# Layer B's attention scores: from 128-row products to pairs of 64-row products

## The chip, the cores and the metric

One core of one Trainium2 chip runs the whole program. The metric is device time in microseconds (us), one launch, the median of the runs. TensorE (PE in the profile) multiplies and loads its weights (PEld), VectorE (DVE), ScalarE (ACT) and GpSimd (POOL) do the rest, and SyncE (SP) issues most of the transfers.

## The reference

Two transformer layers over 512 tokens of width 1024, each with a gate and sandwich norms: layer A is latent attention, layer B differential attention with 8 heads. What matters here is the inner part of layer B. Each head has two halves of 64 dimensions, each half its own scores and its own softmax:

```python
scale = DIFF_QK ** -0.5                       # DIFF_QK = 64
s1 = jnp.einsum('bqhd,bkhd->bhqk', qa, k1).astype(jnp.float32) * scale
s2 = jnp.einsum('bqhd,bkhd->bhqk', qb, k2).astype(jnp.float32) * scale
p = masked_softmax(s1, mask) - lam_full * masked_softmax(s2, mask)
return jnp.einsum('bhqk,bkhe->bqhe', p.astype(v.dtype), v)
```

The mask is causal in chunks of 64 tokens, so a block of 128 queries i needs the keys of the blocks 0 to i only: 128, 256, 384 and 512 of them.

## The kernel before

Every float32 operand is split into a high part and a low remainder (`split`), both in the type that TensorE takes in one pass, and a product is summed from three or four such parts. The layers follow each other: layer A (to about 386 us in the profile), then layer B's attention, then its output projection.

In layer B the query and key projections are made feature-major, split, and stored part by part to two scratch arrays in DRAM, `scratch["q"]` and `scratch["k"]`, with the axes half-head, 64 rows, high or low part, 512 tokens (`to_scratch`). `load_head` (L893) gathers them again. For each half g it loads one tile `q` whose 128 rows are 64 rows of the high and the low part in turn, and two tiles `kh` and `kl`, in which each of the 64 rows of the key's high or low part stands twice. So two products over 128 rows,

```python
pe.matmul(o[:, :n], q[:, ti], kh[:, :n], start=True, stop=False)
pe.matmul(o[:, :n], q[:, ti], kl[:, :n], start=False, stop=True)
```

sum all four part products of one half. `scores_b` (L905) does that for the four query blocks and both halves: 16 products a head, each into a PSUM bank of its own by query block and half, so 8 of the 8 banks pass through a head. The tiles come from a pool `hd` of 8 buffers of 256 KB; a head takes six of them.

`softmax_part` (L515) follows each product with one DVE reduction (L526: mask, scale, copy to SBUF, running extreme, then a short instruction that reads the accumulator into `mx`) and one ACT exponential (L529). `eb`, `mxb` belong to the first half, `ec`, `mxc` to the second. The two halves are combined at L925 and L926.

The order on PE is written out by hand (`pe_order`), the other engines' orders come from the framework's scheduler. `attention_b` (L955) issues the scores of head h+1, then `fill`s of half a projection unit each (12 products of 512 columns) taken from the remaining key, query and gate projections, then the transposes of head h, more fills, the norm's sum of head h-1 (`subln`, a product into the bank `ssb`) and head h's product with the values (`pv`). `BESIDE` says how many half units go where; the first of its three numbers is a `gap` that `softmax_part` calls between the second and the third query block of the scores, so one half unit stands in the middle of a head's scores for heads 1 to 6 (and head 0). Head 7 has none. The weights of the units are split ahead on POOL (high part) and DVE (low part, `wl`, 128x1024); the output projection's second half has the same for `w1h` and `w1l`.

Of the kernel before, what the change touches and what calls it, by code (L numbers as in the profile page):

```python
# [20 lines left out]
P = 128  # L21
# [4 lines left out]
H = 8  # L26
# [3 lines left out]
SCALE_B = 64 ** -0.5  # L30
# [27 lines left out]
def f(ap):  # L58
    return ap.bitcast(F32)
# [84 lines left out]
def body(tc, ins, outs, dbg=None):  # L144
    nc = tc.nc
    ctx = ExitStack()
    with ctx:
        _body(ctx, tc, nc, ins, outs, dbg or {})


def _body(ctx, tc, nc, ins, out, dbg):
# [14 lines left out]
    act, dve, gps, pe = nc.scalar, nc.vector, nc.gpsimd, nc.tensor  # L166

    def ps(name):
        return psp.tile([P, 512], F32, tag="ps", name=name)

    def big_t(name, dt=F32R):
        return big.tile([P, 8, 512], dt, tag="big", name=name)

    def hd_t(name, dt=F32R):
        return hd.tile([P, 512], dt, tag="hd", name=name)

    def tmp_t(name, dt=F32):
        return tmp.tile([P, 512], dt, tag="tmp", name=name)
# [4 lines left out]
    def sm_t(name, n=4, bufs=None):  # L183
        return sm.tile([P, n], F32, tag=name, name=name, bufs=bufs)
# [161 lines left out]
    for kc in range(KC):  # L346
# [4 lines left out]
        g = [ws.get()]  # L351
# [8 lines left out]
        for m in range(5):  # L360
            gh, gl = g[1 if kc == 0 and m else 0]
            k = m - 1 if kc == 0 and m else m
# [74 lines left out]
    for m in range(4):  # L437
        t = tmp_t("cn")
# [38 lines left out]
    for n in range(2):  # L477
        o = [ps(f"va{n}_{i}") for i in range(NT)]
        for p in range(2):
            wh, wl = ws.get()  # L480
            for i in range(NT):
                ti = slice(i * P, i * P + P)
# [29 lines left out]
            qk[nm, h] = (hi, lo)  # L512
        ws.ahead()

    def softmax_part(h, tags, srcs, nscale, gap=None):  # L515

        e = [epool.tile([P, 1280], F32, tag="e", name=f"e{tag}{h}") for tag in tags]
        st = [[sm_t(n + tag) for n in ("mx", "l", "ri")] for tag in tags]
        for i in range(NT):
            n = P * (i + 1)  # L520
            one = slice(i, i + 1)
            for et, (mx, l, _), src in zip(e, st, srcs):
                ev = et[:, OFF[i]:OFF[i] + n]
                o = src(i)

                last = dve.tensor_tensor_reduce(  # L526
                    out=ev, in0=o[:, :n], in1=mask[:, 512 - n:], op0=ALU.add, op1=ALU.min, scalar=-3 * NEG,
                    scale=nscale if isinstance(nscale, float) else nscale[:, one], accum_out=mx[:, one])
                act.activation(ev, ev, AF.Exp, bias=mx[:, one], scale=-1.0, accum_out=l[:, one])  # L529
            if gap and i == 1:  # L530
                gap()
        behind[h] = last.ins
        for _, l, ri in st:
            dve.reciprocal(ri, l)  # L534
        return [(et, x[2]) for et, x in zip(e, st)]
# [26 lines left out]
    def transposes(h):  # L562
        e = es.pop(h)
        b = [ps(f"pt{h}_{k}") for k in range(3)]
        where = [(b[0], 0), (b[1], 0), (b[2], 0), (b[1], 384)]
        for i in range(NT):
            for j in range(i + 1):
                t, o = where[j]
                pe.transpose(t[:, o + (i - j) * P:o + (i - j) * P + P],  # L569
                             e[:, OFF[i] + j * P:OFF[i] + j * P + P], ident)  # L570
        ph = ptp.tile([P, 1280], F32R, tag="pt", name=f"pth{h}")
        pl = ptp.tile([P, 1280], F32R, tag="pt", name=f"ptl{h}")
        for k, (o, n) in enumerate(((0, 512), (512, 512), (1024, 256))):
            split(nc, ph[:, o:o + n], pl[:, o:o + n], b[k][:, :n])
        return ph, pl
# [15 lines left out]
    def split_og(zg, ogh, ogl, hs):  # L591
        for h in hs:
            split(nc, ogh[:, h], ogl[:, h], zg[:, h])
# [51 lines left out]
    def wo_pair(q):  # L645
        w = ws.get()
        for h in (2 * q, 2 * q + 1):
            wo_half0(w, h, range(NT))
        ws.ahead()
        for _ in range(2 if q == 2 else 1):  # L650
            ws.get()
            ws.ahead()
# [175 lines left out]
    scratch = {nm: drp.tile([2 * H, 64, 2, 512], F32, name=f"{nm}dr") for nm in "qk"}  # L828
# [43 lines left out]
    def unit(nm, m):  # L872

        x = (hT1h, hT1l) if nm == "k" else (hT2h, hT2l)
        w = ws.get()
        o = ps(f"{nm}b{m}")
        for kc in range(KC):
            if kc == KC // 2:
                yield
            mm3(o, (w[0][:, kc], w[1][:, kc]), (x[0][:, kc], x[1][:, kc]), kc == 0, kc == KC - 1)  # L880
        ws.ahead()
        evac(nm, m, o)
        yield

    halves = (None for nm, m in beside for _ in unit(nm, m))

    def fill(n):
        for _ in range(n):
            next(halves)

    heads = {}

    def load_head(h, nms="kq"):  # L893
        for g in range(2):
            t = heads.setdefault((h, g), {})
            if "q" in nms:
                t["q"] = hd_t(f"q{g}")
                nc.sync.dma_start(f(t["q"][:]), scratch["q"][2 * h + g].rearrange("r n t -> (r n) t"))
            if "k" in nms:
                for n, nm in enumerate(("kh", "kl")):  # L900
                    t[nm] = hd_t(f"{nm}{g}")
                    nc.sync.dma_start(f(t[nm][:]),
                                      scratch["k"][2 * h + g, :, n].unsqueeze(1).to_broadcast([64, 2, 512]))

    def scores_b(h, gap):  # L905
        hg = [[heads[h, g][nm] for nm in ("q", "kh", "kl")] for g in range(2)]
        second = {}

        def src(i):


            n = P * (i + 1)
            ti = slice(i * P, i * P + P)
            os = [ps(f"sb{h}_{g}_{i}") for g in range(2)]
            for o, (q, kh, kl) in zip(os, hg):
                pe.matmul(o[:, :n], q[:, ti], kh[:, :n], start=True, stop=False)
                pe.matmul(o[:, :n], q[:, ti], kl[:, :n], start=False, stop=True)
            second[i] = os[1]
            return os[0]

        (e1, r1), (e2, r2) = softmax_part(h, "bc", [src, second.get], -SCALE_B, gap)
        dve.tensor_scalar(r2, r2, lam_c, None, op0=ALU.mult)
        for i in range(NT):
            w = slice(OFF[i], OFF[i] + P * (i + 1))
            act.activation(e2[:, w], e2[:, w], AF.Copy, scale=r2[:, i:i + 1])  # L925
            dve.scalar_tensor_tensor(e1[:, w], e1[:, w], r1[:, i:i + 1], e2[:, w],  # L926
                                     op0=ALU.mult, op1=ALU.subtract)
        es[h] = e1
# [3 lines left out]
    def subln_sq(h, o):  # L932
        sq = tmp_t("sqo")
        act.activation(sq, o, AF.Square)
        if h < H - 1:
            ob[h] = tmp_t("sqh", F32R), tmp_t("sql", F32R)
            split(nc, *ob[h], sq)
        else:
            ob[h] = sq,
        dve.scalar_tensor_tensor(zg[:, h], o, gsub, zg[:, h], op0=ALU.mult, op1=ALU.mult)  # L940

    def subln(h):
        b = ps(f"ssb{h}")
        parts = ob.pop(h)
        for n, t in enumerate(parts):
            pe.matmul(b, ones_r if len(parts) > 1 else ones, t, start=n == 0, stop=n == len(parts) - 1)
        rs = tmp_t("rs")
        act.activation(rs, b, AF.Ln, bias=eps_c, scale=1.0 / 128)
        act.activation(rs, rs, AF.Exp, scale=-0.5)
        (dve if h > 4 else gps).tensor_tensor(zg[:, h], zg[:, h], rs, op=ALU.mult)  # L950


    BESIDE = [(1, 2, 2), (1, 2, 3), (1, 2, 1), (1, 2, 2), (1, 1, 1), (1, 1, 2), (0, 0, 0)]

    def attention_b():  # L955
        pt = {}
        scores_b(0, lambda: fill(1))
        load_head(1)
        fill(4)
        for h in range(H):  # L960
            a, b, c = BESIDE[h] if h + 1 < H else (0, 0, 0)
            if h + 1 < H:
                scores_b(h + 1, lambda: fill(a))
                fill(b)
                if h + 2 < H:
                    load_head(h + 2)
            if h == 5:
                st["og"] = big_t("ogh"), big_t("ogl")
            if h == 6:
                w1[0], w1[1] = st["w1"] = big_t("w1h"), big_t("w1l")  # L970
                st["acc"] = [ps(f"wo0_{i}") for i in range(NT)]
                wo_pair(0)
            pt[h] = transposes(h)
            fill(c)
            if h == 6:
                subln(5)
                split_og(zg, *st["og"], [5])
                wo_pair(1)
            elif h == 7:
                wo_pair(2)  # L980
            elif h:
                subln(h - 1)
                if h == 5:
                    split_og(zg, *st["og"], range(5))
            subln_sq(h, pv(h, pt.pop(h)))
# [117 lines left out]
```

## Time and profile before

| what | value |
|---|---|
| median of 3 runs | 578.09 us (578.03 to 578.71) |
| the profiled execution | 576.0 us, of which the span from first to last instruction is 574.1 us |
| granted TensorE clock | 0.998 over the span; 1.00 from 386 to 535 us |
| DVE, ACT, POOL busy | 63%, 44%, 24% of the span |
| layer B's score products | 386.2 to 515 us, 128 products |

A row of the timeline has the start and the length of an instruction in us, its engine, line, operation, the tiles it writes and reads, and shapes. PE's products overlap: what one costs in a dense stretch is the distance from its start to the next start, not its length. A bracket gives the idle time before it and who ended it.

### The profile page before, as it was taken

Reading aid. Unit: us, or ns where it says so; the run is one execution under the profiler, and the core shown is the slowest. Engines: PE = TensorE matmul, PEld = TensorE weight load, DVE = VectorE, ACT = ScalarE, POOL = GpSimd, SP = SyncE. Lnnn points to the kernel's source line nnn. Section 1 sums busy time; section 2 is a strip of 40 time slices with the busy share of each in tenths; the row PEclk is TensorE's granted clock in tenths of the full one; section 3 lists DMA queues with packets and bytes.
Section 4 is the critical chain, followed back from the end, with each engine's and each line's share of the span. In section 5 each row is a group of like instructions: output and inputs, shape, how many; then the busy total and the mean of one; then the engine's idle time right before and its main releaser. Section 6 shows DMA issues by size and latency. Waiting matters only on the chain.

```text
span 574.1 us, 7800 instructions
## 1 busy us (share of the span) xinstructions
PE 565.5 (98%) x2749; PEld 477.4 (83%) x2749; DVE 362.5 (63%) x728; ACT 252.0 (44%) x560; POOL 139.9 (24%) x191
## 2 busy tenths in 40 slices
PE   8999999999999999999999999999999999999995
PEld 7888888888888888888888888888888888888785
DVE  6839845335566665856786575436666667687554
ACT  6146152222244344331476130124674695986432
POOL 1044402012232323321122332332223223243000
PEclk9999999999999999999999999999999999999999
DMA  8356576655544335697741377845755745557012
GB/s 303 104 180 184 185 231 192 217 165 132 168 131 125 97 104 165 208 375 259 237 147 47 110 202 224 288 130 189 250 172 179 238 130 181 187 168 253 1 58 90
DMA packets 39334, 100.54 MB, mean 175 GB/s; under 512 B 4592, under 2 KB 5248, under 8 KB 39296
## 3 DMA queue, kind: packets, MB, share of 16 engines
q1 hardware_dynamic: 26048, 57.16, 29.2%
q0 software_dynamic: 12624, 41.97, 24.4%
q10 hardware_dynamic: 624, 0.92, 0.6%
q8 instruction: 22, 0.36, 0.3%
q14 instruction: 16, 0.13, 0.1%
HBM read 86.66 MB, written 12.58 MB: 173 GB/s over the span
## 4 chain that ended last, share of the span: by engine, by line
PE 90%; DMA 3%; issue 2%; DVE 2%; POOL 1%; ACT 0%; DVEq 0%; POOLq 0%
PE wo L194 4%; PE wo L192 4%; PE wo L193 4%; PE za L192 3%; PE zb L192 3%; PE zb L193 3%; PE qb L194 3%; PE kb L193 3%; PE kb L194 3%; PE kb L192 3%; PE qb L193 3%; PE vb L194 3%; PE za L193 3%; PE vb L193 3%; PE vb L192 3%; PE za L194 3%
## 5 line engine op out<-in xcount | busy, mean ns | idle before, releaser
L116 DVE TENSOR_TENSOR wl<-wr,wh 128x1024 fp32r<-128x1024 f32 (+2 forms) x44 | 46.9, 1067 | 50.7 <-DMA wh<-in_w_uv 7.5
L138 POOL TENSOR_SCALAR wh<-wr 128x1024 fp32r<-128x1024 f32 x30 | 33.4, 1113 | 78.3 <-PE zb L193 26.7
L141 DVE TENSOR_TENSOR wl<-wr,wh 128x1024 fp32r<-128x1024 f32 x32 | 39.0, 1219 | 17.1 <-POOL wh L138 17.0
L136 ACT ACTIVATE pth<-pt 128x512 fp32r<-128x512 f32 (+1 forms) x48 | 22.3, 525 | 17.6 <-PE pt L569 17.4
L141 DVE TENSOR_TENSOR ptl<-pt,pth 128x512 fp32r<-128x512 f32 (+1 forms) x48 | 26.3, 593 | 4.2 <-ACT pth L136 3.8
L529 ACT ACTIVATE ea<-ea,mxa 128x128 f32<-128x128 f32 (+3 forms) x32 | 18.0, 561 | 22.9 <-DVE mxa L526 22.8
L557 POOL TENSOR_SCALAR ea<-ea,ria 128x128 f32<-128x128 f32 (+3 forms) x32 | 16.9, 541 | 41.7 <-DVE ria L534 41.7
L192 PE MATMUL wo<-w1h,ogh 128*128 128x512 f32 (+1 forms) x72 | 26.8, 372 | 0.0
L193 PE MATMUL wo<-w1l,ogh 128*128 128x512 f32 (+1 forms) x72 | 26.4, 367 | 0.0
L194 PE MATMUL wo<-w1h,ogl 128*128 128x512 f32 (+1 forms) x72 | 26.4, 366 | 0.0
L194 PE MATMUL wo<-wh,ogl 128*128 128x512 f32 x64 | 24.9, 392 | 0.3 <-DVE ogl L141 0.3
L192 PE MATMUL zb<-hT2h,wh 128*128 128x512 f32 x64 | 25.3, 395 | 0.0
L192 PE MATMUL kb<-hT1h,wh 128*128 128x512 f32 x64 | 25.1, 393 | 0.0
L193 PE MATMUL wo<-wl,ogh 128*128 128x512 f32 x64 | 25.0, 391 | 0.0
L192 PE MATMUL za<-xh,wh 128*128 128x512 f32 x64 | 25.0, 391 | 0.0
L194 PE MATMUL zb<-hT2h,wl 128*128 128x512 f32 x64 | 25.0, 391 | 0.0
L192 PE MATMUL qb<-hT2h,wh 128*128 128x512 f32 x64 | 25.0, 391 | 0.0
L193 PE MATMUL zb<-hT2l,wh 128*128 128x512 f32 x64 | 25.0, 390 | 0.0
L194 PE MATMUL qb<-hT2h,wl 128*128 128x512 f32 x64 | 24.9, 390 | 0.0
L193 PE MATMUL kb<-hT1l,wh 128*128 128x512 f32 x64 | 24.9, 390 | 0.0
L194 PE MATMUL kb<-hT1h,wl 128*128 128x512 f32 x64 | 24.9, 390 | 0.0
L193 PE MATMUL qb<-hT2l,wh 128*128 128x512 f32 x64 | 24.9, 389 | 0.0
(347 smaller groups left out, 1707.4 us busy)
## 6 DMA issues: line engine op xcount, KB each, us to landing
wr<-in_w_za SPq DMA_DIRECT2D x8, 512.0 KB, 3.9
wh<-in_w_za POOLq DMA_DIRECT2D x8, 512.0 KB, 4.2
wr<-in_w_oa SPq DMA_DIRECT2D x8, 512.0 KB, 4.4
wr<-in_w_qb POOLq DMA_DIRECT2D x8, 512.0 KB, 5.1
kh<-kdr SPq DMA_DIRECT2D x16, 256.0 KB, 4.0
kl<-kdr SPq DMA_DIRECT2D x16, 256.0 KB, 4.0
q<-qdr SPq DMA_DIRECT2D x16, 256.0 KB, 3.7
wr<-in_w_zb POOLq DMA_DIRECT2D x8, 512.0 KB, 3.9
```

What stands on the lines that cost most here:

```text
L116: self.nc.vector.tensor_tensor(lo, raw, f(hi), op=ALU.subtract)
L136: nc.scalar.activation(hi, src, AF.Copy)
L138: nc.gpsimd.tensor_scalar(hi, src, 1.0, 1.0, op0=ALU.mult, op1=ALU.mult)
L141: (nc.vector if lo_eng == "dve" else nc.gpsimd).tensor_tensor(lo, src, f(hi), op=ALU.subtract)
L192: pe.matmul(o, w[0], x[0], start=first, stop=False)
L193: pe.matmul(o, w[0], x[1], start=False, stop=False)
L194: pe.matmul(o, w[1], x[0], start=False, stop=last)
L529: act.activation(ev, ev, AF.Exp, bias=mx[:, one], scale=-1.0, accum_out=l[:, one])
L557: gps.tensor_scalar(ev, ev, ri[:, i:i + 1], 1.0, op0=ALU.mult, op1=ALU.mult)
```

## The change

`load_head` loads plain rows: per head two tiles for q and two for k, one of the high and one of the low parts, with half 0 in rows 0 to 63 and half 1 in rows 64 to 127. `scores_b` makes three products a query block and half (high by high, low by high, high by low; the product of the two low parts is no longer summed), each over 64 rows, the two halves in turn: half 0 on the rows 0 to 63 of the array, half 1 on the rows 64 to 127. The products of the query blocks 0 and 1 (128 and 256 columns) of a half share one PSUM bank, `two[g]`, so a head takes six banks. The gap is gone: a head's four query blocks follow each other, and `BESIDE` keeps the number of fills between one head's scores and the next.

```diff
-    def softmax_part(h, tags, srcs, nscale, gap=None):
+    def softmax_part(h, tags, srcs, nscale):
...
-            if gap and i == 1:
-                gap()
...
     def load_head(h, nms="kq"):
-        for g in range(2):
-            t = heads.setdefault((h, g), {})
-            if "q" in nms:
-                t["q"] = hd_t(f"q{g}")
-                nc.sync.dma_start(f(t["q"][:]), scratch["q"][2 * h + g].rearrange("r n t -> (r n) t"))
-            if "k" in nms:
-                for n, nm in enumerate(("kh", "kl")):
-                    t[nm] = hd_t(f"{nm}{g}")
-                    nc.sync.dma_start(f(t[nm][:]),
-                                      scratch["k"][2 * h + g, :, n].unsqueeze(1).to_broadcast([64, 2, 512]))
-
-    def scores_b(h, gap):
-        hg = [[heads[h, g][nm] for nm in ("q", "kh", "kl")] for g in range(2)]
-        second = {}
+
+        t = heads.setdefault(h, {})
+        for nm in nms:
+            src = scratch[nm][2 * h:2 * h + 2].rearrange("g r n t -> (g r) n t")
+            t[nm] = hd_t(f"{nm}h"), hd_t(f"{nm}l")
+            for n in range(2):
+                nc.sync.dma_start(f(t[nm][n][:]), src[:, n])
+
+    def scores_b(h):
+        t = heads.pop(h)
+        (qh, ql), (kh, kl) = t["q"], t["k"]
+        halves = [slice(64 * g, 64 * g + 64) for g in range(2)]
+        second, two = {}, [ps(f"sb{h}_{g}_01") for g in range(2)]
...
-            os = [ps(f"sb{h}_{g}_{i}") for g in range(2)]
-            for o, (q, kh, kl) in zip(os, hg):
-                pe.matmul(o[:, :n], q[:, ti], kh[:, :n], start=True, stop=False)
-                pe.matmul(o[:, :n], q[:, ti], kl[:, :n], start=False, stop=True)
+            os = [two[g][:, P * i:P * i + n] if i < 2 else ps(f"sb{h}_{g}_{i}")[:, :n] for g in range(2)]
+            for a, (q, k) in enumerate(((qh, kh), (ql, kh), (qh, kl))):
+                for o, rs in zip(os, halves):
+                    pe.matmul(o, q[rs, ti], k[rs, :n], start=a == 0, stop=a == 2)
...
-    BESIDE = [(1, 2, 2), (1, 2, 3), (1, 2, 1), (1, 2, 2), (1, 1, 1), (1, 1, 2), (0, 0, 0)]
+    BESIDE = [(3, 2), (3, 3), (3, 1), (3, 2), (2, 1), (2, 2), (0, 0)]
...
-        scores_b(0, lambda: fill(1))
+        scores_b(0)
         load_head(1)
-        fill(4)
+        fill(5)
...
-                scores_b(h + 1, lambda: fill(a))
-                fill(b)
+                scores_b(h + 1)
+                fill(a)
```

On PE only the score products change their place and number; every other PE instruction keeps its order. The first place is PE at the scores of head 0, query blocks 0 and 1 (`sb_0` and `sb_1` are the two halves' banks, the bracket names what an instruction waits for). Before:

```order
L916 MATMUL sb_0_0_3414<-kh_3102,q_3270 128x128 [waits DMAHW2_49,DMAHW0_49]
L917 MATMUL sb_0_0_3414<-kl_3104,q_3270 128x128 [waits DMAHW3_49]
L916 MATMUL sb_1_0_3415<-kh_3106,q_3272 128x128 [waits DMAHW4_49,DMAHW1_49]
L917 MATMUL sb_1_0_3415<-kl_3108,q_3272 128x128 [waits DMAHW5_49]
L916 MATMUL sb_0_1_3424<-kh_3102,q_3270 128x256
L917 MATMUL sb_0_1_3424<-kl_3104,q_3270 128x256
L916 MATMUL sb_1_1_3425<-kh_3106,q_3272 128x256
L917 MATMUL sb_1_1_3425<-kl_3108,q_3272 128x256
```

After this, half a unit of `kb` followed. With the change:

```order
L913 MATMUL sb_0_01_3402<-kh,qh 128x128 [waits DMAHW6_49,DMAHW2_49]
L913 MATMUL sb_1_01_3403<-kh,qh 128x128
L913 MATMUL sb_0_01_3402<-kh,ql 128x128 [waits DMAHW7_49]
L913 MATMUL sb_1_01_3403<-kh,ql 128x128
L913 MATMUL sb_0_01_3402<-kl,qh 128x128 [waits DMAHW3_49]
L913 MATMUL sb_1_01_3403<-kl,qh 128x128
L913 MATMUL sb_0_01_3402<-kh,qh 128x256 [waits DVE_49]
L913 MATMUL sb_1_01_3403<-kh,qh 128x256 [waits DVE_49]
L913 MATMUL sb_0_01_3402<-kh,ql 128x256
L913 MATMUL sb_1_01_3403<-kh,ql 128x256
L913 MATMUL sb_0_01_3402<-kl,qh 128x256
L913 MATMUL sb_1_01_3403<-kl,qh 128x256
```

Eight products have become twelve, in pairs, and the first 256-column product of each half now waits for DVE, in head 0 as in every head. By the semaphore's count in the built program it is the accumulator read (`mxb`, and `mxc` for the second half) of the reduction of query block 0, which reads the same bank.

The second place is DVE at the scores of head 7 with the change. These rows stood in the same order before:

```order
L141 TENSOR_TENSOR w1l<-wr_4661,w1h 128x1024
L141 TENSOR_TENSOR w1l<-wr_4861,w1h 128x1024
L526 ISA eb_4768,mxb<-sb_0_01_4766,mask 128x128
L526 ISA mxb 128x1
L526 ISA ec_4769,mxc<-sb_1_01_4767,mask 128x128
L526 ISA mxc 128x1
L526 ISA eb_4768,mxb<-sb_0_01_4766,mask 128x256
```

Nothing moved here; two splits of the output projection's weights stand ahead of the reductions, and PE now waits for the second and the fourth of the rows after them.

## Rows read from the trace of the kernel before

**Rows 1.** The page, busy time by engine, and the chain's shares by engine.
```profile
PE 565.5 (98%) x2749; PEld 477.4 (83%) x2749; DVE 362.5 (63%) x728; ACT 252.0 (44%) x560; POOL 139.9 (24%) x191
...
PE 90%; DMA 3%; issue 2%; DVE 2%; POOL 1%; ACT 0%; DVEq 0%; POOLq 0%
```

**Rows 2.** The view of waits, PE alone: us in total, times, longest.
```profile
PE warm L291 <- DVE ones L279: 1.1, 1, 1.1
PE g L366 <- ACT xh L348: 0.5, 1, 0.5
PE wo L194 <- DVE ogl L141: 0.3, 1, 0.3
PE sa L194 <- DVE qnl L141: 0.2, 1, 0.2
```

**Rows 3.** Timeline of PE, head 1's scores: where each query block starts.
```profile
402.43 0.22 PE L916 MATMUL sb<-kh,q 128*128 128x128 f32 x1
...
402.83 0.33 PE L916 MATMUL sb<-kh,q 128*128 128x256 f32 x1
...
403.35 0.40 PE L192 MATMUL zb<-hT2h,wh 128*128 128x512 f32 x1
...
406.10 0.33 PE L916 MATMUL sb<-kh,q 128*128 128x384 f32 x1
...
406.81 0.40 PE L916 MATMUL sb<-kh,q 128*128 128x512 f32 x1
...
407.73 0.40 PE L192 MATMUL zb<-hT2h,wh 128*128 128x512 f32 x1
```

**Rows 4.** Timeline of PEld, head 0: weight loads of 128-column products.
```profile
386.34 0.19 PEld L916 LDWEIGHTS sb<-kh,q 128*128 128x128 f32 x1
...
386.45 0.19 PEld L917 LDWEIGHTS sb<-kl,q 128*128 128x128 f32 x1
```

**Rows 5.** Timeline, head 0: first half's last 128-column product, then both reductions.
```profile
386.29 0.28 PE L917 MATMUL sb<-kl,q 128*128 128x128 f32 x1
...
386.60 0.29 DVE L526 CUSTOM_DVE_ANT_0 eb<-sb,mask 128x128 f32<-128x128 f32 x1 [0.21 <-PE sb L917]
...
386.82 0.09 DVE L526 DVE_READ_ACCUMULATOR2_ANT mxb<- 128x1 f32 x1
...
387.04 0.08 DVE L526 DVE_READ_ACCUMULATOR2_ANT mxc<- 128x1 f32 x1
```

**Rows 6.** Timeline, output projection: a PE product released by DVE.
```profile
533.41 0.40 PE L193 MATMUL wo<-wl,ogh 128*128 128x512 f32 x1
...
533.41 0.68 DVE L141 TENSOR_TENSOR ogl<-zb,ogh 128x512 fp32r<-128x512 f32 x1
...
534.15 0.50 PE L194 MATMUL wo<-wh,ogl 128*128 128x512 f32 x1 [0.34 <-DVE ogl L141]
```

**Rows 7.** Timeline, head 7: the splits on DVE, the first product, the first reduction.
```profile
510.90 3.20 DVE L141 TENSOR_TENSOR w1l<-wr,w1h 128x1024 fp32r<-128x1024 f32 x2 [1.31 <-POOL w1h L138]
...
512.13 0.28 PE L916 MATMUL sb<-kh,q 128*128 128x128 f32 x1
...
514.02 0.28 DVE L526 CUSTOM_DVE_ANT_0 eb<-sb,mask 128x128 f32<-128x128 f32 x1
```

**Rows 8.** The chain that ended last, 510 to 534 us: its longest pieces.
```profile
514.40 6.26 DMA wr<-in_w_ob
...
521.72 6.81 DMA wr<-in_w_ob
...
533.49 0.61 DVE ogl L141
```

**Rows 9.** Timeline of PE: ten transposes between units, an edge of another kind of product.
```profile
412.97 0.39 PE L194 MATMUL zb<-hT2h,wl 128*128 128x512 f32 x1
413.20 1.25 PE L569 MATMUL pt<-ident,eb 128*128 128x128 f32 x10
414.21 0.48 PE L192 MATMUL kb<-hT1h,wh 128*128 128x512 f32 x1
414.52 0.39 PE L193 MATMUL kb<-hT1l,wh 128*128 128x512 f32 x1
```

More of the change, by code (lines that the diff above doesn't have):

```diff
@@ L913, in src @@
             ti = slice(i * P, i * P + P)
-            os = [ps(f"sb{h}_{g}_{i}") for g in range(2)]
-            for o, (q, kh, kl) in zip(os, hg):
-                pe.matmul(o[:, :n], q[:, ti], kh[:, :n], start=True, stop=False)
-                pe.matmul(o[:, :n], q[:, ti], kl[:, :n], start=False, stop=True)
+            os = [two[g][:, P * i:P * i + n] if i < 2 else ps(f"sb{h}_{g}_{i}")[:, :n] for g in range(2)]
+            for a, (q, k) in enumerate(((qh, kh), (ql, kh), (qh, kl))):
+                for o, rs in zip(os, halves):
+                    pe.matmul(o, q[rs, ti], k[rs, :n], start=a == 0, stop=a == 2)
             second[i] = os[1]
             return os[0]
-        (e1, r1), (e2, r2) = softmax_part(h, "bc", [src, second.get], -SCALE_B, gap)
+        (e1, r1), (e2, r2) = softmax_part(h, "bc", [src, second.get], -SCALE_B)
         dve.tensor_scalar(r2, r2, lam_c, None, op0=ALU.mult)
@@ L950, in subln @@
         (dve if h > 4 else gps).tensor_tensor(zg[:, h], zg[:, h], rs, op=ALU.mult)
-    BESIDE = [(1, 2, 2), (1, 2, 3), (1, 2, 1), (1, 2, 2), (1, 1, 1), (1, 1, 2), (0, 0, 0)]
+    BESIDE = [(3, 2), (3, 3), (3, 1), (3, 2), (2, 1), (2, 2), (0, 0)]
     def attention_b():
         pt = {}
-        scores_b(0, lambda: fill(1))
+        scores_b(0)
         load_head(1)
-        fill(4)
+        fill(5)
         for h in range(H):
-            a, b, c = BESIDE[h] if h + 1 < H else (0, 0, 0)
+            a, b = BESIDE[h] if h + 1 < H else (0, 0)
             if h + 1 < H:
-                scores_b(h + 1, lambda: fill(a))
-                fill(b)
+                scores_b(h + 1)
+                fill(a)
                 if h + 2 < H:
@@ L973, in attention_b @@
             pt[h] = transposes(h)
-            fill(c)
+            fill(b)
             if h == 6:
```

## The prediction

> **What bounds the kernel now.** I read the page first: PE is busy 98% of the span and carries 90% of the chain that ended last [rows 1]. Then the waits of PE: four in the whole program, 2.1 us together, and none in front of a score product [rows 2]. So wherever PE's stream grows or shrinks between 386 and 510 us, the end moves by as much. The third view is PE's timeline at one head's scores. The row starts give prices: four products of 128 columns take 402.83 - 402.43 = 0.40 us, four of 256 take 0.52, four of 384 take 0.71, four of 512 take 0.92 [rows 3], which is 0.10, 0.13, 0.18 and 0.23 us each and 2.55 us a head. A product of 128 columns is hardly cheaper than one of 256, since a weight load comes only every 0.11 us [rows 4]. Fourth, DVE's timeline at the same place, because the change makes PE wait for it [rows 5 to 7]. Last, the chain late in layer B: from 514 to 534 us it leaves PE and goes through two weight transfers and DVE [rows 8], so PE has a little slack there.
>
> **What the change saves on PE.** Sixteen products of 128 rows a head become 24 of 64 rows, twelve pairs. If the two of a pair stream side by side on their halves of the array, a query block takes three slots where it took four. No row shows a 64-row product, so the slot's price is bounded: below by that of one full product of the same width (side by side), above by two of them (one after the other). I take the lower, since the two touch neither the same rows of the array nor the same bank, and both operands of a pair are there at once. That makes 3/4 of 2.55 = 1.91 us a head, 0.64 less, and 8 heads save 5.1 us.
>
> **What the new wait costs.** Query blocks 0 and 1 of a half now share a bank, and the first 256-column product of each half waits for the reduction of the 128-column one. Nothing else stands on PE to fill this: PE is in order, and the gap unit that stood in the scores has gone behind them. The round trip, from the start A of the last pair of block 0: the product ends at A + 0.28 (a 128-column product's length); the reductions of the two halves then start 0.03 later, and the second half's accumulator read ends 0.55 after the product's end (386.57 to 387.12) [rows 5]; PE starts 0.06 after DVE's end (534.09 to 534.15) [rows 6]. Together A + 0.89. The first half's product may go some 0.2 us sooner, but its own next product stands behind the second half's. Without the wait the next pair would start at A + 0.10, so a head loses 0.79 us and 8 heads 6.3 us. The bounds: from below 0.28 + 0.03 + 0.31 + 0.06 - 0.10 = 0.58 us, if only the first half's release counted; from above, a split of weights that happens to stand ahead on DVE.
>
> **Head 7.** Here such a split does stand ahead. DVE is busy with the two `w1l` splits until 514.02 and only then reduces the first product [rows 7], which with the change would be ready at 512.13 + 0.20 + 0.28 + 0.03 = 512.64. Before, PE did not care: it went on with its other banks. Now it waits 1.4 us more. Of this, about 0.5 us costs nothing: PE waited at the edge at 534 us for DVE anyway (a distance of 0.74 us where 0.23 is normal) [rows 6], behind transfers that the scores of head 7 do not release [rows 8]. Net + 0.9 us.
>
> **Switching between full and half rows.** 16 times, at either side of a head's scores. The lower bound is nothing: transposes follow a unit's product at the ordinary 0.23 us. The upper is that the earlier product must have run out: 0.39 long less 0.23 distance = 0.16 us. Between them lies the other edge of the transposes, where the next product is at a distance of 0.31, 0.08 more than usual [rows 9]; it is the nearest, since there too the kind of product changes, and I take it: 16 x 0.08 = 1.3 us. The Trainium skill, page "TensorEngine Tiling (Array Packing)", section "Key Properties", says that changing the tiling mode drains TensorE, which speaks against the change. By that rule the upper bound holds, 16 x 0.16 = 2.6 us, and the sum would be 1.3 us higher; by the row it stays as it is.
>
> **What costs nothing.** Six loads of 256 KB a head become four, on SP; no product waited for one before [rows 2], and with four of eight buffers a head the loads for head h+2 wait for head h's scores, no longer for head h+1's. If that cover were gone, a head would start late by part of a transfer. The gap's half unit only moves behind the scores, with the same number of fills before the next head's, so key and query projections are stored no later relative to their use. The reductions of one head now arrive with no unit between them; six banks hold them while PE does two or three half units, so they need not be ready sooner. The low-by-low products are in the saving already.
>
> **The sum.** - 5.1 + 6.3 + 0.9 + 1.3 = + 3.4 us. The profiled execution took 576.0 us and would take 579.4; the median of the runs is 2.1 us above it, so the forecast is 578.1 + 3.4 = 581.5 us. By the bounds of this case alone (wait 0.58 to 0.9 us a head, a switch at 0 to 0.16) it is + 0.4 to + 5.6 us.
>
> **The rivals.** *The pair is bound by its weight loads.* Every product loads 128 columns of weights. A load comes every 0.11 us [rows 4]; if the loads of the two halves go one after the other, a pair costs 0.22 us at 128, 256 and 384 columns and 0.23 at 512, a head 3 x 0.89 = 2.67 instead of 1.91 us, and 8 heads lose 6.1 us more: 587.6 us. For it: the row that shows 128 columns bound by the load. Against: each half has its own rows to load. The Trainium skill, page "TensorE: Matmul & The Clock Gate", section "LDWEIGHTS (loading the stationary operand)", counts a load by its columns, not its rows, so that halving the rows would make it no cheaper; no run here shows a 64-row load.
>
> *The pair does not run side by side at all*, so that the change does not do what it says: 24 products at full price, 3.83 us a head, 1.92 x 8 = 15.3 us over the forecast, 596.8 us. For it: nothing in this trace shows two products at once; the overlap of their lengths is a pipeline's. Against: no shared rows, no shared bank. The Trainium skill, page "TensorE: Matmul & The Clock Gate", section "Part 3: Packing small matmuls — row/col tiling", lets products on different row groups start within about 4 ns of each other, which would rule this rival out; no row here shows it.
>
> *The wait hardly binds, and the kernel gets faster.* The order names the engine that PE waits for, not how long. If DVE's release comes at the time PE gets there, by a shorter pass through 64 rows or because PE has work in flight, the wait term goes to 0 and with it head 7's: - 5.1 + 1.3 = - 3.8, 574.3 us. It turns at a wait of (5.1 - 1.3) / 8 = 0.47 us a head. Against it: what is waited for is the reduction of the product just issued, and the product's tail, DVE's two reductions and their reads are 0.83 us in the rows [rows 5].
>
> **How the numbers follow.** The forecast's case gets 0.55: most of it slower, some 0.13 of it within 0.2% (1.2 us, about what a measurement of this kernel can tell from no change), where the wait and the switches lie at their lower bounds. The weight loads get 0.25, the serial pair 0.10, the wait that does not bind 0.10, of which 0.02 is within 0.2%. So faster 0.08, same 0.15, slower 0.77. The range leaves out the serial case and the fast one, and reaches from the forecast's lower bound, 0.4 above the median less a margin for the median itself (577.8), to the weight-load case with some lateness of DVE (589.0).
>
> **What would show it.** Right: in each head PE idle before the first 256-column score products, released by DVE's `mxb` and `mxc`, some 0.8 us together and over 2 us in head 7; pairs of score products starting almost together, pair to pair at 0.10 to 0.23 us by width; the edges at 0.08 us over the usual distance. Pairs 0.22 us apart at 128 columns mean weight loads; starts at full distances mean serial pairs. The prediction is wrong if that wait is missing from the view of waits, or if PE stands at another place: at a bank, at a load of a head, or at the weights after head 7.

## The result and the profile after

| | before | after |
|---|---|---|
| median of 4 runs each, on the same chip | 578.06 us (576.57 to 578.71) | 585.59 us (584.84 to 586.75) |
| ratio | | 1.0121 [1.0089, 1.0153] |
| the profiled execution, its span | 576.0, 574.1 us | 586.0, 584.2 us |

A bracket behind a ratio is its 95% interval. Medians are of all runs of a kernel; ratios and intervals leave out the few runs that lie over 1.5% above the fastest of the same kernel.

The kernel became slower by 7.5 us; the forecast was 581.5 in a range of 577.8 to 589.0. Direction and range held, the size was twice too small. The page of the changed kernel, busy time and the chain's shares, against [rows 1]:

```profile
PE 568.5 (97%) x2813; PEld 475.7 (81%) x2813; DVE 366.6 (63%) x728; ACT 251.9 (43%) x560; POOL 139.2 (24%) x191
...
PE 84%; DMA 5%; DVE 4%; issue 3%; POOL 2%; ACT 1%; ACTq 0%; DVEq 0%; POOLq 0%
```

PE's share of the chain fell from 90% to 84%; DVE and DMA took most of it. The view of waits, PE alone (us in total, times, longest), against [rows 2], says where:

```profile
PE sb L913 <- DVE mxb L526: 4.9, 8, 2.1
PE o L193 <- DVE ptl L141: 1.3, 1, 1.3
```

Eight waits before score products, one a head, as forecast, and one late in the program that was not. No product waits for a load of a head, so the four plain loads cost nothing here.

To compare stages I cut PE's timeline at three row starts: head 0's first score product, head 7's first, and the first product after head 7's scores; the end is the start of PE's last product. All rows are from one profiled execution each, in us:

| kernel | heads 0 to 6 | head 7's scores | rest | together |
|---|---|---|---|---|
| before | 125.90 | 2.80 | 52.33 | 181.03 |
| before, a second trace | 125.88 | 2.80 | 51.66 | 180.34 |
| after | 129.69 | 5.95 | 53.61 | 189.25 |
| after, a second trace | 129.64 | 5.12 | 53.58 | 188.34 |

The spans differ by 10.1 us, these parts by 8.2. The other 1.8 us lie ahead of head 0 (it starts at 388.07, before at 386.23), where PE has the same instructions in both. The second trace of before starts head 0 at 388.94, so this is scatter and not the change's.

**Head 0.** PE's timeline of after, against [rows 3]; `x2` is a pair of which the row gives the first start, and the whole length:

```profile
388.07 0.33 PE L913 MATMUL sb<-kh,qh 64*128 64x128 f32 x2
388.24 0.28 PE L913 MATMUL sb<-kh,ql 64*128 64x128 f32 x2
388.35 0.27 PE L913 MATMUL sb<-kl,qh 64*128 64x128 f32 x2
389.01 0.59 PE L913 MATMUL sb<-kh,qh 64*128 64x256 f32 x2 [0.39 <-DVE mxb L526]
...
391.00 0.50 PE L192 MATMUL kb<-hT1h,wh 128*128 128x512 f32 x1
```

A pair starts 0.11 us after the one ahead (388.24 to 388.35) and lasts 0.27, as one full product of 128 columns did: the two run side by side. The weight loads do so too, in PEld's timeline of the same place, against [rows 4]:

```profile
388.18 0.19 PEld L913 LDWEIGHTS sb<-kh,ql 64*128 64x128 f32 x2
388.29 0.19 PEld L913 LDWEIGHTS sb<-kl,qh 64*128 64x128 f32 x2
```

Two loads in 0.19 us, a pair every 0.11, where one load stood every 0.11. Then comes the wait. DVE's timeline, against [rows 5]:

```profile
388.66 0.29 DVE L526 CUSTOM_DVE_ANT_0 eb<-sb,mask 128x128 f32<-128x128 f32 x1 [0.52 <-PE sb L913]
388.88 0.08 DVE L526 DVE_READ_ACCUMULATOR2_ANT mxb<- 128x1 f32 x1
...
389.09 0.08 DVE L526 DVE_READ_ACCUMULATOR2_ANT mxc<- 128x1 f32 x1
```

With A = 388.35, the first half's accumulator read ends at 388.96 and PE's 256-column product starts at 389.01 = A + 0.66. The second half's read ends at 389.17 = A + 0.82; its product can only follow then, which is why the pair's row is 0.59 long where a pair without a wait takes 0.33 (experiment 2). The row ends at 389.60, and a single 256-column product behind such a wait lasts 0.38 (experiment 5), so the second one starts at about 389.22 = A + 0.87. Forecast was A + 0.89. The 0.39 in the bracket is only PE's idle time, less than what the wait costs, since the last products' lengths cover the start of it and the second half's lateness shows in no bracket.

**Head 7.** PE's timeline:

```profile
518.03 0.28 PE L913 MATMUL sb<-kl,qh 64*128 64x128 f32 x2
520.41 0.79 PE L913 MATMUL sb<-kh,qh 64*128 64x256 f32 x2 [2.10 <-DVE mxb L526]
...
522.17 0.84 PE L913 MATMUL sb<-kh,qh 64*128 64x512 f32 x2
522.60 0.84 PE L913 MATMUL sb<-kh,ql 64*128 64x512 f32 x2
...
523.71 0.50 PE L192 MATMUL wo<-wh,ogh 128*128 128x512 f32 x1
```

And what DVE did meanwhile, against [rows 7]:

```profile
518.92 1.23 DVE L141 TENSOR_TENSOR w1l<-wr,w1h 128x1024 fp32r<-128x1024 f32 x1 [1.26 <-POOL w1h L138]
520.06 0.28 DVE L526 CUSTOM_DVE_ANT_0 eb<-sb,mask 128x128 f32<-128x128 f32 x1
```

The first product was ready for DVE at about 518.34; DVE idled for 1.26 us for POOL, did the split that stands ahead, and reduced at 520.06, 1.7 us late. PE's distance from the last 128-column pair to the next is 2.38 us; in head 0, with its wait, it is 0.66. What follows is slow as well: the 512-column pairs stand 0.43 us apart (522.17 to 522.60), in head 0 it is 0.23. The windows of PE there (busy, the granted clock, DMA share, GB/s) give the reason:

```profile
519.00:520.00 1.00, 0.00 (x0) 1.00 0.00 0
520.00:521.00 1.00, 0.59 (x3) 0.57 0.61 98
521.00:522.00 1.00, 1.00 (x10) 0.50 1.00 406
523.00:524.00 1.00, 1.00 (x6) 0.72 0.79 311
```

After 2.1 us of idling PE is granted the lower of its two levels, 1.2 GHz, to about 523.5. From the first 256-column product to the end of the scores it takes 523.71 - 520.41 = 3.30 us; in head 0, at a clock of 1.00, the same takes 391.00 - 389.01 = 1.99. So the clock costs 1.3 us.

**The end.** The chain that ended last, after head 7, and PE's row where it comes back to PE, against [rows 6, 8]:

```profile
520.45 4.58 DMA wr<-in_w_ob
...
526.45 5.90 DMA wr<-in_w_ob
...
533.51 0.83 DVE w1l L141
...
537.32 0.61 DVE ptl L141
```

```profile
537.97 0.50 PE L193 MATMUL o<-ptl,vhb 128*128 128x512 f32 x1 [1.29 <-DVE ptl L141]
```

As before two transfers of weights and splits on DVE are on the chain, and PE waits for DVE at its end: now 1.29 us for `ptl`, where it was 0.34 for `ogl`.

### The profile page after: what moved, and what is told of

It reads as the page before. It is cut to its first block, busy times and chain, and to the rows that moved or that the text cites. A ratio compares the mean times of both kernels' runs of the same rounds, so it can differ in the third digit from the quotient of the medians.

```text
span 584.2 us, 7886 instructions
## 1 busy us (share of the span) xinstructions
PE 568.5 (97%) x2813; PEld 475.7 (81%) x2813; DVE 366.6 (63%) x728; ACT 251.9 (43%) x560; POOL 139.2 (24%) x191
## 4 chain that ended last, share of the span: by engine, by line
PE 84%; DMA 5%; DVE 4%; issue 3%; POOL 2%; ACT 1%; ACTq 0%; DVEq 0%; POOLq 0%
PE wo L192 4%; PE wo L193 4%; PE wo L194 4%; PE sb L913 3%; PE kb L192 3%; PE qb L192 3%; PE kb L194 2%; PE qb L194 2%; PE vb L194 2%; PE vb L192 2%; PE kb L193 2%; PE qb L193 2%; PE vb L193 2%; PE pt L567 2%; DMA wr<-in_w_ob 2%
## 5 line engine op out<-in xcount | busy, mean ns | idle before, releaser
L194 PE MATMUL za<-xh,wl 128*128 128x512 f32 x64 | 25.0, 391 | 0.2 <-DVE wl L116 0.2
```

The source lines that it names most:

```text
L194: pe.matmul(o, w[1], x[0], start=False, stop=last)
```

## The experiments

Medians and ratios are against the kernel before on the same chip. The parts are those of the table above.

**1. Only the order of the query blocks.** Blocks 2 and 3, in banks of their own, go between the two that share one.

```diff
-        (e1, r1), (e2, r2) = softmax_part(h, "bc", [src, second.get], -SCALE_B)
+        (e1, r1), (e2, r2) = softmax_part(h, "bc", [src, second.get], -SCALE_B, (0, 2, 3, 1))
```

(`softmax_part` loops over this tuple in place of `range(NT)`.)

> The changed kernel with the query blocks taken in the order 0, 2, 3, 1, so that three pairs of 384 and three of 512 columns stand between the first user of a shared bank and the second. Theory (the wait behind the shared bank costs 0.55 us a head in heads 0 to 6, 2.3 us and a clock drop of 1.3 us in head 7): PE no longer waits at mxb in heads 0 to 6 and less than 1 us in head 7, and the time falls by 5 to 7 us, to 579 to 581 us. Rival (the cost is the edges between 128-row and 64-row products, the wait is small change): no edge is taken away, the time stays at 584 to 586 us.

Measured: 577.72 us (12 runs), before 578.01 (35 runs), 0.9991 [0.9956, 1.0025]. Parts 123.85, 3.51, 52.83. The waits of PE:

```profile
PE sb L913 <- DVE mxb L526: 0.9, 1, 0.9
PE o L193 <- DVE ptl L141: 0.5, 1, 0.5
```

The wait of heads 0 to 6 is gone, one of 0.9 us in head 7 is left. Heads 0 to 6 are 129.69 - 123.85 = 5.84 us shorter than after, 0.83 a head, and head 7's scores 2.44. The 7.9 us between the two medians, more than the 5 to 7 expected, come from nothing but the order of four blocks.

**2. Every block a bank of its own**, otherwise as after:

```diff
-        second, two = {}, [ps(f"sb{h}_{g}_01") for g in range(2)]
+        second = {}
...
-            os = [two[g][:, P * i:P * i + n] if i < 2 else ps(f"sb{h}_{g}_{i}")[:, :n] for g in range(2)]
+            os = [ps(f"sb{h}_{g}_{i}")[:, :n] for g in range(2)]
```

> The changed kernel with a bank of its own for every query block and half, eight a head, still without the gap. Theory: the wait for mxb is gone in all heads, 577 to 580 us; some 0.2 to 0.5 us a head may come back as a wait for a bank that the value product or the norm still holds. Rival (the missing gap packs the reductions so that PE runs into DVE whatever the banks): the waits move from mxb of block 0 to later reductions with about the same sum, 583 to 586 us.

Measured: 578.08 us (10 runs), 1.0017 [0.9989, 1.0044]. Parts 123.78, 3.77, 53.84. Heads 0 to 6 are the same as in experiment 1 within 0.07 us, so it is the shared bank and not the order that cost them. In head 7 PE now waits 1.2 us for a bank to come free, for the same DVE instruction. And this timeline shows the edges without a wait between them (head 1):

```profile
405.88 0.39 PE L194 MATMUL zb<-hT2h,wl 128*128 128x512 f32 x1
406.19 0.33 PE L913 MATMUL sb<-kh,qh 64*128 64x128 f32 x2
406.36 0.28 PE L913 MATMUL sb<-kh,ql 64*128 64x128 f32 x2
406.47 0.27 PE L913 MATMUL sb<-kl,qh 64*128 64x128 f32 x2
406.58 0.33 PE L913 MATMUL sb<-kh,qh 64*128 64x256 f32 x2
406.75 0.28 PE L913 MATMUL sb<-kh,ql 64*128 64x256 f32 x2
406.87 0.28 PE L913 MATMUL sb<-kl,qh 64*128 64x256 f32 x2
...
407.17 0.34 PE L913 MATMUL sb<-kh,ql 64*128 64x384 f32 x2
407.34 0.34 PE L913 MATMUL sb<-kl,qh 64*128 64x384 f32 x2
...
407.74 0.40 PE L913 MATMUL sb<-kh,ql 64*128 64x512 f32 x2
407.98 0.40 PE L913 MATMUL sb<-kl,qh 64*128 64x512 f32 x2
408.30 0.50 PE L192 MATMUL zb<-hT2h,wh 128*128 128x512 f32 x1
408.64 0.39 PE L193 MATMUL zb<-hT2l,wh 128*128 128x512 f32 x1
```

Entry: 0.31 where 0.23 is normal, then 0.17 where the next pairs have 0.11. Exit: 0.32 and 0.34 where 0.23 is normal. From the first pair to the unit this head takes 408.30 - 406.19 = 2.11 us, where the prediction counted 1.91; with the 0.08 ahead of it and the 0.11 behind it that makes 0.39 us for its two edges. (The first 256-column pair, 0.17 from the next, is no edge: before has 0.17 there too, 402.83 to 403.00.)

**3. Experiment 2, with the gap back.** The half unit stands in the middle of the scores again, with the old `BESIDE`, so a head has two entries and two exits.

```diff
+            if gap and i == 1:
+                gap()
...
-    BESIDE = [(3, 2), (3, 3), (3, 1), (3, 2), (2, 1), (2, 2), (0, 0)]
+    BESIDE = [(1, 2, 2), (1, 2, 3), (1, 2, 1), (1, 2, 2), (1, 1, 1), (1, 1, 2), (0, 0, 0)]
```

> 64-row pairs in the schedule of the kernel before: a bank for each query block and half, and the half unit in the middle of the scores of heads 0 to 6. Theory (an entry and an exit between 128-row and 64-row products cost 0.4 us together): seven more entries and exits than with separate banks and no gap, so 2.5 to 3 us more than that run, about 581 us, and no wait on PE in the scores. Rival (the edges are cheap): within 1 us of that run.

Measured: 580.77 us (10 runs), 1.0045 [1.0011, 1.0079]. Parts 126.82, 3.22, 53.76. No score product of heads 0 to 6 waits. Against experiment 2, heads 0 to 6 grow by 3.04 us, 0.43 for each entry and exit more. So two entries and two exits a head are enough to turn the saving of the pairs into a loss: against before, heads 0 to 6 are 0.92 us longer, with no shared bank at all. One of the added exits:

```profile
404.94 0.28 PE L915 MATMUL sb<-kl,qh 64*128 64x256 f32 x2
405.15 0.50 PE L192 MATMUL zb<-hT2h,wh 128*128 128x512 f32 x1
405.49 0.39 PE L193 MATMUL zb<-hT2l,wh 128*128 128x512 f32 x1
```

0.21 and 0.34 us, where a 256-column pair takes 0.12 and a product of a unit 0.23.

**4. The shared bank alone**: before's loads (left out below) and 128-row products, with after's `two` and its order without a gap.

```diff
...
-            for a, (q, k) in enumerate(((qh, kh), (ql, kh), (qh, kl))):
-                for o, rs in zip(os, halves):
-                    pe.matmul(o, q[rs, ti], k[rs, :n], start=a == 0, stop=a == 2)
+            for o, (q, kh, kl) in zip(os, hg):
+                pe.matmul(o, q[:, ti], kh[:, :n], start=True, stop=False)
+                pe.matmul(o, q[:, ti], kl[:, :n], start=False, stop=True)
```

> The 128-row products of the kernel before, but with query blocks 0 and 1 in one bank and without the gap: the wait alone, with no pair and no edge. Theory: 0.4 to 0.6 us in heads 0 to 6 and 2 to 4 us in head 7 over the kernel before, 583 to 586 us. Rival (the edges are the cost): at the kernel before, 577 to 579 us.

Measured: 582.3 us (10 runs), 1.0067 [1.0038, 1.0096]. Parts 128.73, 4.43, 52.45. Heads 0 to 6 are 2.83 us longer than before, 0.40 a head, and head 7's scores 1.63, less than the 2 to 4 expected. The 0.40 is half of the 0.83 that the wait costs with pairs. With 128-row products half 0 is done two products ahead of half 1, and in head 0 its first 256-column product starts 0.45 us after the last 128-column one (387.45 to 387.90). Half 0's second one follows at 388.12, and by half 1's turn at 388.24 its reduction, done at 388.06, is no longer waited for. In a pair both halves end together, and nothing is left to run beside the second reduction. This run also separates the wait from the clock. Its wait in head 7 is 1.6 us long, and the windows of PE show the clock staying up:

```profile
PE sb L914 <- DVE mxb L526: 3.1, 8, 1.6
```

```profile
517.00:518.00 1.00, 0.00 (x0) 1.00 0.00 0
518.00:519.00 1.00, 0.87 (x6) 1.00 0.67 98
```

**5. One half after the other** in the program: three products of half 0, then three of half 1.

```diff
-            for a, (q, k) in enumerate(((qh, kh), (ql, kh), (qh, kl))):
-                for o, rs in zip(os, halves):
+            for o, rs in zip(os, halves):
+                for a, (q, k) in enumerate(((qh, kh), (ql, kh), (qh, kl))):
```

> The changed kernel with the three products of half 0 ahead of the three of half 1, instead of in turn, so that neighbours stand on the same rows of the array. Theory (two products run at once only where neighbours lie on different rows): most of the overlap goes, four of six slots in place of three at best where the halves meet, six at worst, so 0.6 to 1.9 us a head, and the time rises by 5 to 15 us, to 590 to 600 us. Rival (the array finds the other half's products further down the stream): no change, 584 to 587 us.

Measured: 586.03 us (one run, before 577.28). Parts 129.65, 5.71, 52.81: no difference from after in heads 0 to 6. My theory that the halves share the array only if their products alternate in the program fell. PE's timeline in head 1:

```profile
406.88 0.38 PE L913 MATMUL sb<-kh,qh 64*128 64x256 f32 x1 [0.38 <-DVE mxb L526]
...
407.35 0.34 PE L913 MATMUL sb<-kh,qh 64*128 64x384 f32 x1
407.42 0.44 PE L913 MATMUL sb<-kh,ql 64*128 64x256 f32 x2
407.54 0.28 PE L913 MATMUL sb<-kl,qh 64*128 64x256 f32 x1
```

In the program all 256-column products stand ahead of all 384-column ones. By the records a 384-column product starts at 407.35, ahead of 256-column ones at 407.42 and 407.54. So the half that is released first runs ahead, and the other follows at its own pace. In head 7 PE idles for 1.8 us, and the granted clock falls to 0.50 behind that too (521.35 to 524.76 us). The Trainium skill, page "TensorE: Matmul & The Clock Gate", section "Part 3: Packing small matmuls — row/col tiling", says that products start and end strictly in program order, also when they are packed; the rows here differ, and the rows decide.

**6. Banks of their own in head 7 alone:**

```diff
-            os = [two[g][:, P * i:P * i + n] if i < 2 else ps(f"sb{h}_{g}_{i}")[:, :n] for g in range(2)]
+            os = [two[g][:, P * i:P * i + n] if i < 2 and (h < 7 or i == 0) else ps(f"sb{h}_{g}_{i}")[:, :n] for g in range(2)]
```

> The changed kernel with separate banks for query blocks 0 and 1 in head 7 alone. Theory: heads 0 to 6 as in the changed kernel; in head 7 the idle time of 2.1 us becomes about 1.2 us at a later bank, as in the run with separate banks, and PE's clock does not drop there, so 2 to 3 us less than the changed kernel: 582 to 584 us. Rival (the end of layer B is set by the weight transfers whatever head 7 does): 585 to 586 us.

Measured: 583.42 us (4 runs), 1.0117 [1.0053, 1.018]. Parts 129.64, 3.66, 54.04. Head 7 gives back 5.95 - 3.66 = 2.29 us: its longest wait is now 1.0 us, at the last block, and the clock stays at 1.00. Heads 0 to 6 are as in after. The rest is not shorter: PE waits 1.7 us for `ptl`.

**7. to 9. Taking the wait of head 7 away from the kernel of experiment 1.** `wo_pair(0)` issues the first pair of the output projection's heads, with the work on its weights. Experiment 7 moves the split that stands ahead of head 7's reductions behind the first of them (`began[7]`, the reduction of block 0), 8 puts one of the half units behind head 7's scores, and 9 moves the split behind all of head 7's reductions (`behind[7]`):

```diff
+            if i == 0:
+                began[h] = last.ins
...
-                wo_pair(0)
+                with tc.issue_after(began[7]):
+                    wo_pair(0)
```

```diff
-    BESIDE = [(3, 2), (3, 3), (3, 1), (3, 2), (2, 1), (2, 2), (0, 0)]
+    BESIDE = [(3, 2), (3, 3), (3, 1), (3, 2), (2, 1), (2, 1), (1, 0)]
```

```diff
-                wo_pair(0)
+                with tc.issue_after(behind[7]):
+                    wo_pair(0)
```

> The order 0, 2, 3, 1 and, in addition, the first product with the output weights, with all that it splits and loads, issued on the other engines only after head 7's reductions of block 0, so that no split of weights stands ahead of them on DVE. Theory: the last wait in the scores (0.9 us in head 7) goes, 575 to 577.5 us, if the later splits do not come too late for the output projection. Rival (the splits are needed as early as they stand): PE waits for them or for the transposes' remainders instead, 578 to 580 us.

> The order 0, 2, 3, 1 with the last half unit of the gate projection moved behind head 7's scores. Theory: the buffer that the output weights go to comes free later, so their splits start behind head 7's reductions and PE does not wait in the scores; but the chain of transfers behind them starts about 4 us later and PE meets it near the end of layer B: 576 to 579 us, with a wait of 0.5 to 3 us that was not there. Rival (those transfers have slack): 575 to 576.5 us.

> The order 0, 2, 3, 1, and the first product with the output weights issued on the other engines only after all of head 7's reductions. Theory: neither the wait for block 0 nor the wait of the output projection for a bank (0.8 us in the run before this) is left, 179 us from the first score product to PE's last one and 575 to 577.5 us in all. Rival (the output weights' splits are then late): a wait of 1 us or more for a split or for the transposes' remainders, 578 to 580 us.

| | median, runs | ratio to before | heads 0 to 6 | head 7's scores | rest |
|---|---|---|---|---|---|
| 7 | 577.56, 12 | 0.9996 [0.9965, 1.0026] | 123.86 | 2.11 | 53.87 |
| 8 | 578.02, 12 | 1.0011 [0.9974, 1.0047] | 123.24 | 2.11 | 55.63 |
| 9 | 580.72, 12 | 1.004 [1.0005, 1.0074] | 123.87 | 2.11 | 57.13 |

Experiment 8's first and last part can't be set beside the others': one half unit, 12 products or 2.75 us by [rows 3], has moved from the one to the other. In all three, head 7's scores take 2.11 us, like head 1's in experiment 2, and the time comes back elsewhere. Experiment 8 came out as expected, 7 just above its 575 to 577.5 us with a wait that neither its theory nor its rival had; in 9 the theory fell, and 580.72 us lies even above the rival's 578 to 580. In 7 the output projection waits for the bank instead:

```profile
PE wo L192 <- DVE mxb L526: 0.8, 1, 0.8
```

In 8 the half unit taken from ahead of head 7 had covered head 5's transposed attention weights: PE waits 0.3 us for `pth` and 1.0 for `ptl` at its product with the values, just ahead of head 7, and 0.7 for `ptl` at 537 us. In 9 PE waits 1.6 us for `ptl`, the longest time 1.26 us up to 529.54, and 0.7 for `ogh`, and is granted a clock of only 0.87 and 0.91 in the windows of 8 us from 524 and from 532. A window of 1 us in between:

```profile
530.00:531.00 1.00, 1.00 (x7) 0.50 0.88 352
```

None of these kernels beats before by more than its interval.

**10. Before and after once more**, unchanged, for a second trace of each.

> The kernel before once more, for a second trace. If the part from the first score product to PE's last product is steady and the spread between runs lies ahead of it, that part takes 180.5 to 181.6 us again (181.0 in the first trace), while the start of the scores may lie anywhere between 386 and 390 us.

> The changed kernel once more, for a second trace. The same part takes 188.5 to 190 us again (189.25 in the first), with waits of 0.55 us in heads 0 to 6, about 2 us in head 7, and PE at half its clock behind that one.

Measured: 578.02 and 584.34 us, one run each. The three parts together, 180.34 and 188.34 us, lie 0.2 us below what was expected. The stages agree with the first traces to 0.05 us in heads 0 to 6; the slow clock comes again, in other products. The windows of PE in the second trace of after, whose wait in head 7 was 2.3 us long:

```profile
520.00:521.00 1.00, 1.00 (x13) 1.00 0.79 324
521.00:522.00 1.00, 1.00 (x8) 0.70 1.03 229
523.00:524.00 1.00, 1.00 (x4) 0.50 0.98 395
```

Here the scores keep 1.00 at first and the fall, some 1.6 us after PE's restart, hits the last of them and the units behind them: so head 7 is shorter than in the first trace, and the rest is as long as there though no wait for `ptl` stands in it.

## Why the prediction was right or wrong

The terms of its sum, and what the runs give for each:

| step of the prediction | forecast | measured | from |
|---|---|---|---|
| pairs | - 5.1 | - 5.1 | distances in experiment 2 |
| wait, 8 heads | + 6.3 | + 6.7 | 5.84 / 7 x 8, after against experiment 1 |
| switches | + 1.3 | + 2.8 to 3.1 | 0.35 or 0.39 a head, below |
| head 7, lateness of DVE | + 1.4 | + 1.7 | 2.38 - 0.66, against head 0 |
| head 7, slack at 534 us | - 0.5 | 0 | not given back; it would lie in the rest |
| the clock | none | + 1.3 | 3.30 - 1.99 |
| the rest | 0 | + 1.3 | 53.61 - 52.33 |
| sum | + 3.4 | + 8.7 to 9.0 | 8.2 between the traces from head 0 on, 7.5 between the medians |

The terms come to some 0.5 us more than the traces differ by. In head 7 of before the scores took 2.80 us and not the 2.55 of the price, so pairs and edges together gave 2.80 - 2.11 = 0.69 us there, and not 0.25 to 0.3.

**What the change saves on PE: right.** Pairs start 0.11, 0.12, 0.17 and 0.23 us apart at 128, 256, 384 and 512 columns, the price of one full product each. The rivals of the serial pair and of the weight loads fall: 0.11 us at 128 columns is neither 0.20 nor 0.22, and two loads of 64 rows take the 0.19 us of one.

**What the new wait costs: right.** 0.79 us forecast, 0.83 measured by taking the wait away in two different ways (experiments 1 and 2). The mechanism is the one worked out, too: what counts is the second half's release, A + 0.87 in head 0 against A + 0.89. The fast rival, where the wait hardly binds, needed less than 0.47 us a head. It was nearer than I saw: with 128-row products the same wait costs 0.40 (experiment 4), and only in a pair, where both halves end together, is it 0.83.

**Switching: the step that was too small.** I took 0.08 us for an edge, from the transposes, and 0.16 as the upper bound. Heads 0 to 6 of experiment 1 are 125.90 - 123.85 = 2.05 us shorter than before, where the pairs alone would save 0.64 x 7 = 4.48; 2.43 us went into 7 heads, 0.35 a head or about 0.17 an edge. The rows of one head in experiment 2 give 0.39, experiment 3 gives 0.43 for one more entry and exit. The error was in what I let an edge be: one longer distance. That distance is as forecast, 0.08 and 0.09 longer at entry and exit. In the rows there are two at either side, the switch and the product behind it (0.32 and 0.34 at the exit). The Trainium skill, page "TensorEngine Tiling (Array Packing)", section "Key Properties", has changing the mode drain the engine; by it I would have taken the upper bound, 2.6 us, close to what was measured. Whether the engine drains these rows do not show: the starts lie 0.31 and 0.32 apart, while the product ahead lasts 0.39 and 0.40 by the record, whose ends are modelled. The nearest row was not near: a transpose is another kind of product, but it stays on all 128 rows.

**Head 7: half right.** The wait came as worked out, a split on DVE ahead of the first reduction, 1.7 us late in place of 1.4: by then DVE had itself waited for POOL. Two things followed that the sum did not have. First, after this idle time the granted clock fell, in both traces of after, and in the first of them the products at the lower clock cost 1.3 us. Second, the 0.5 us of slack did not help. I had read [rows 6] as a wait that stays in place while head 7 gets later. It needs the weights' transfers to keep their times, and they do not: a transfer starts 0.3 to 0.4 us after a `w1l` split ends (514.10 to 514.40 us before, by [rows 7, 8]; about 520.06 to 520.45 after), and the split itself was 6.0 us later than before, head 7's start 5.6. The chain moved along with PE. Besides, the second trace of before has no such wait and a rest of 51.66 instead of 52.33 us, so the slack was one execution's, not the kernel's. How much of the + 1.3 us in the rest is scatter of this kind stays open: the rest differs by 0.67 us between the two traces of before, and lies at 52.4 to 54.0 in experiments 1 to 7.

**What costs nothing: right.** No wait for a load of a head, and the reductions that arrive without a unit between them are covered by six banks: apart from the shared bank no score product of heads 0 to 6 waits.

So the direction rested on the right mechanism, saving and wait of about the same size with the edges on top. The miss, 4.1 us between the medians and 4.8 between the traces, is the edges (some 1.6 us) and, above all, what follows the wait in head 7: the clock (1.3), the slack that was counted and not there (0.5), and the longer rest (1.3, of which the share of scatter is open). By the forecast's own bounds, + 0.4 to + 5.6 us, it would have been 583.7 us at most. The measured 585.59 lies in the stated range only because that reaches up to the weight-load rival, and that rival fell: here the range held by luck.

## What to carry to other kernels

Packing two tiles into one bank made PE wait here for the reader of the first tile, although the columns differ; put other work between the two users of a bank (here the order 0, 2, 3, 1 gave back 7.9 us) before counting what the packing saves. Count the edges of row-tiled products, some 0.35 us for an entry and an exit here, against the slots saved, 0.64 us a head, and make one run of such products rather than two. And look at a wait's longest case before its sum: the one of 2.1 us here cost the clock as well.

## What was not expected of the hardware

Products on different halves of the array did not keep program order between them: in experiment 5 a 384-column product started ahead of 256-column ones that stand before it, and the time was that of the alternating order (586.03 and 585.59 us). The weight loads of the two halves ran at the same time as well, two in 0.19 us.

The granted clock fell to 0.50 after idle times of PE of 2.1 and 2.3 us (the two traces of after), of 1.8 us (experiment 5) and of 1.26 us (experiment 9): within the idle time in the first trace, some 0.2 to 0.4 us after PE had started again in experiments 5 and 9, some 1.6 us after it in the second trace. It stayed at 1.00 after idle times of 1.4 us (experiment 3), 1.5 us (experiment 2), 1.6 us (experiment 4) and 1.7 us (experiment 6). So the length of one idle time alone does not tell here whether the clock falls; what else decides it these runs do not show.

With the same instructions ahead of it, layer B's first score product started between 386.2 and 390.2 us in the traces of this study. A difference of two spans of this kernel means little below some 4 us unless the stages are cut apart.
